# Moving a convolution's norm and a branch's product along a stick-breaking attention kernel, with some sums done by accumulating DMA

## The chip, the cores and the metric

The kernel runs on one core of a Trainium2 chip. The metric is device time in microseconds (us), the median over runs of one launch. The engines are called by their names in the profile: PE (TensorE, matrix products), DVE (VectorE), ACT (ScalarE), POOL (GpSimd) and SP (SyncE, which here only issues DMAs). All times are of the whole launch or of places in the span of one profiled execution.

## The reference, cut

One layer on `x` of 2048 rows by 1024 channels: a layer norm, one wide product with `w_in` into nine blocks of 1024 columns, then two branches that meet.

```python
h = _layer_norm(x, ln_in_g, ln_in_b)
q, k, v, z_sb, c_val, c_gate, z_cv, g_sb, g_cv = split(h @ w_in)          # 9 x 1024 columns
# branch s: 16 heads of 64; A[t,s] = sigmoid(l_ts) * prod_{s<j<t} (1 - sigmoid(l_tj)), s < t
y_sb = (attention(q, k, v) * silu(z_sb)) @ w_sb_proj
# branch c: causal depthwise convolution of 31 taps, layer norm over channels
u = conv(c_val * sigmoid(c_gate), conv_w, conv_b)
y_cv = (silu(_layer_norm(u, conv_ln_g, conv_ln_b)) * silu(z_cv)) @ w_cv_proj
merged = sigmoid(g_sb) * y_sb + sigmoid(g_cv) * y_cv
out = _layer_norm(ALPHA * h + merged @ w_out, ln_g, ln_b)
```

## The kernel before, in words

The rows are turned end to start, so that the attention's running products go forward; they are held as four chunks of 512 rows. Half 1 is chunks 3 and 2, half 0 chunks 1 and 0. Channels lie on the 128 partitions, in eight blocks. Every fp32 operand of a product is split into a high part `hi` (ScalarE, `activation` Copy to fp32r, L116) and a low part `lo` (VectorE, source minus `hi`, L117), and a product is three matmuls, `hi*hi`, `hi*lo`, `lo*hi`. A piece of work for PE in the fill lists is two of eight blocks of the contraction, so six matmuls of 512 columns; four pieces make one tile of 128 x 512, and `block` is two such tiles, one for each chunk of a half.

The first phase computes most column blocks of `h @ w_in` by a scheme of seven products in place of eight (L909). Its work comes in groups of 14 pieces: `order(h)` lists them, 36 groups for half 1 and 20 for half 0. A group `u` gives the gated input of one channel block of the convolution; when both chunks are there, `gated` queues a convolution (a generator of 51 steps, 45 of them taps of VectorE at L409) on the list `slow`.

`slow_step` is called after every piece. It adds `PACES[phase]` to a counter and, where the counter has reached 1, runs one step of the first convolution in the list, at a priority lowered by 800.

The convolution's norm is `conv_mean(h)` (mean over channels by a product with `ones`) and `conv_ln(c)`: for each of eight channel blocks subtract the mean, square and sum (`s2`, L467 to L474), then the inverse root through POOL (`m2`, `m3`), then scale, SiLU and the gate (`s3`, L501 to L505), into `acv`.

The second phase is the attention of eight pairs of heads, for half 1 and then for half 0, woven with a list of fill pieces: for each pair `k`, `q`, `v` and the gate `z` of half 0 (`fill_qkv`, `gate_z`), then branch `s` of half 1, then branch `c` of half 1. `weave_attention` orders the attention's items: logits (L583, L584), sigmoid (L586), a scan on VectorE (L589), a turn (four transposes at L612, split by L116 and L117), the product with `v` (L628). `SPLIT` is the share of the fill that lies beside half 1's attention, and `END` the number of entries of the fill that are left when the attention's last item has been issued. `done` closes a head: it sums the two halves of the partitions (L642), adds `v` (L648), multiplies by the gate (L649) and stores into `asb`.

The tail runs branch `s` of half 0, the output rows of chunks 3 and 2, branch `c` of half 0, and the output rows of chunks 1 and 0. `pair` interleaves the first two and last two blocks of a branch and lets `freed` start the loads of the next operands; `load_w` loads and splits a block's weights, or reads back split parts where an earlier pass has stored them (`wdr`). `soon` and `delay` put an item into the fill after a number of further entries.

Issue order on PE is the program's order. The other engines' order is made by the scheduler from priorities, but each engine then runs its own queue in order. All DMAs are issued from SP's queue.

The branch's end, as it stands (L707 to L717):

```python
def use(c, ps, g, *a):
    o = st()
    nc.vector.tensor_tensor(out=o, in0=ps, in1=g, op=ALU.mult)
    for a_ in a:
        nc.vector.tensor_tensor(out=o, in0=o, in1=a_, op=ALU.add)
    dma((mdr if a else pdr)[c, m], o)
```

Of the kernel before, what the change touches and what calls it, by code (L numbers as in the profile page):

```python
# [27 lines left out]
NBW = 4  # L28
LEAD = 4.0
LAG = 3  # L30
PACES = [0.78, 1.25, 0.6]
I0 = 1
SPLIT = 0.27
RD = 9
W1 = 5
END = 14
W0 = 3
N1 = 2
O0 = 25
O1 = 5  # L40
B0 = 62
# [13 lines left out]
def layer_kernel(ctx: ExitStack, tc, x, w_in, w_sb, w_cv, w_out, vecs, cw, rows, out):  # L55
# [32 lines left out]
    def dram(shape, dt, name):  # L88
        return tc.dram_tile(shape, dt, name=name)
# [7 lines left out]
    asb = {(c, m): dram([P, CH], F32, f"asb{c}_{m}") for c, m in CM}  # L97
    acv = {(c, m): dram([P, CH], F32, f"acv{c}_{m}") for c, m in CM}
    mdr = {(c, m): dram([P, CH], F32, f"mdr{c}_{m}") for c, m in CM}
    pdr = {(c, m): dram([P, CH], F32, f"pdr{c}_{m}") for c, m in CM}  # L100
    qdr = {(c, m): dram([2, P, CH], F32R, f"qdr{c}_{m}") for c, m in CM}
    kdr = {(c, m): dram([2, P, CH], F32R, f"kdr{c}_{m}") for c, m in CM}
    vtd = {(c, m): dram([P, CH], F32, f"vtd{c}_{m}") for c, m in CM}
# [40 lines left out]
    def load_w(src, col):  # L144


        hi, lo = (wp.tile([P, KB, P], F32R, name="w4", bufs=4) for _ in range(2))
        for g in range(2):
            ks = slice(g * 4, g * 4 + 4)
            if (id(src), col, g) in wdr:  # L150
                for t, e in ((hi, 0), (lo, 1)):
                    dma(t[:, ks], wdr[id(src), col, g][:, e])
                continue
            raw = wp.tile([P, 4, P], F32, name="wraw", bufs=2)
            nc.sync.dma_start(out=raw, in_=src[col // P][:, ks])
            split(raw, hi[:, ks], lo[:, ks])
        return hi, lo

    class Fill:
# [83 lines left out]
    def half(h):  # L243
        return (2 * h + 1, 2 * h)
# [268 lines left out]
    def attention(at, kv, lg_p, pv_p):  # L513
# [123 lines left out]
        def done(i, a, c, ps, hs, ls):  # L637
            if a == 0:
                sums[c] = at.tile([P, CH], F32, name="og", bufs=2)
            g, s = sums[c], st()  # L640
            nc.scalar.activation(s[hs], ps[ls], AF.Copy)
            nc.vector.tensor_tensor(out=g[hs], in0=ps[hs], in1=s[hs], op=ALU.add)  # L642
            if a == 0:
                return
            v, z = st(), st()
            dma(v, vtd[c, i])
            dma(z, gat[c, i, "b"])
            nc.vector.tensor_tensor(out=g, in0=g, in1=v, op=ALU.add)  # L648
            nc.vector.tensor_tensor(out=g, in0=g, in1=z, op=ALU.mult)  # L649
            dma(asb[c, i], g)  # L650

# [41 lines left out]
    def branch(n, h):  # L693

        def gate(m):
            def load(c):
                g = sg_p.tile([P, CH], F32, name="gt", bufs=2)
                dma(g, gat[c, m, n])
                return g
            return load  # L700

        def other(m):
            def load(c):
                a = st()
                dma(a, pdr[c, m])
                return a
            return load  # L707

        def use(m):
            def use(c, ps, g, *a):  # L710
                o = st()
                nc.vector.tensor_tensor(out=o, in0=ps, in1=g, op=ALU.mult)  # L712
                for a_ in a:
                    nc.vector.tensor_tensor(out=o, in0=o, in1=a_, op=ALU.add)
                dma((mdr if a else pdr)[c, m], o)
            return use

        src, bys = (w_sb, [gate]) if n == "s" else (w_cv, [gate, other])
        return [(src, m * P, [(c, lambda c=c: acts[n, c]) for c in half(h)], use(m)) + tuple(b(m) for b in bys)
                for m in range(KB)]  # L720

    srcs = {"s": asb, "c": acv, "m": mdr}
# [18 lines left out]
    def first_phase(F, x2, w1, ps_p):  # L741
# [255 lines left out]
            return g  # L997

        def order(h):
            us_ = [("u", m) for m in range(KB)]  # L1000
            rest = [(e, m) for m in range(4) for e in ("kqvzcgh" if h else "cgh")]
            out_ = []
            for n, u in enumerate(us_):
                out_.append(u)
                out_ += rest[len(rest) * n // 8:len(rest) * (n + 1) // 8]
            return out_

        groups = [group(1, *o) for o in order(1)] + [group(0, *o) for o in order(0)]
        rows, one, two = first_rows()
# [9 lines left out]
        later_rows()  # L1019
        prev, prev_g = None, None  # L1020
        for n, g in enumerate(groups):
            nxt = groups[n + 1] if n + 1 < len(groups) else None
            last = nxt is None or nxt["h"] != g["h"]
            first = n == 0
# [123 lines left out]
    with ExitStack() as s2:  # L1148
        kv = s2.enter_context(tc.tile_pool(name="kv", bufs=2))
        at = s2.enter_context(tc.tile_pool(name="at", bufs=2))  # L1150
        lg_p = s2.enter_context(tc.tile_pool(name="lgp", bufs=2, space=PS))
        pv_p = s2.enter_context(tc.tile_pool(name="pvp", bufs=2, space=PS))
        head = attention(at, kv, lg_p, pv_p)

        def gate_z(m):
            return w_in, COL_Z + m * P, xs(0), silu_to(m, "b")

        for i in range(NPAIR):
            ready[1, i] = True
        norm = conv_mean(1) + conv_ln(3) + conv_ln(2)  # L1160
        for i in range(NPAIR):
            fill_qkv(F, 0, i)
            if i < NPAIR - 2:
                F.block(*gate_z(i))
            for q in range(10):
                if norm and i >= I0:
                    F.delay(1 + 3 * q, 0.1, norm.pop(0))
        F.pair(gate_z(NPAIR - 2), gate_z(NPAIR - 1), freed=loads("s", 1))
        F.soon([(0.1, it) for it in norm], 1, 2)
        run(F, branch("s", 1), loads("c", 1))  # L1170
        F.soon([(0.1, it) for it in conv_mean(0) + conv_ln(1) + conv_ln(0)], N0, N1)
        run(F, branch("c", 1), loads("s", 0))
        end = len(F.pieces) - END
        steps, spans = [], []
        mid = int(end * SPLIT)
        for h, lo, hi in ((1, 0, mid), (0, mid, end)):
            spans += [(lo + (hi - lo) * i // NPAIR, lo + (hi - lo) * (i + 1) // NPAIR) for i in range(NPAIR)]
            for i in range(NPAIR):
                for a in range(2):
                    steps += [((0 if h else NPAIR) + i, st_) for st_ in head(i, a, h)]  # L1180
        pair_of = [p_ for p_, _ in steps]
        items = weave_attention([st_ for _, st_ in steps])
        work = {}
        for n, _, (cost, _) in items:
            work[pair_of[n]] = work.get(pair_of[n], 0) + cost
        seen = {}
        at_fill = 0
        for n, own, (cost, fn) in items:
            p_ = pair_of[n]
            lo, hi = spans[p_]  # L1190
            k = seen.get(p_, 0)
            seen[p_] = k + cost
            at_fill = max(at_fill, lo + int((hi - lo) * k / work[p_]))
            emit_fill(at_fill)
            o_ = pair_of[own]
            while (1 - o_ // NPAIR, o_ % NPAIR) not in ready:
                at_fill = n_done[0] + 1
                emit_fill(at_fill)
            fn()


    with ExitStack() as s2:
# [72 lines left out]
                            F.soon(freed)  # L1275

        run(F, branch("s", 0), loads("m", 1))
        output(F, 3, loads("c", 0)[0])
        output(F, 2, loads("c", 0)[1])
        run(F, branch("c", 0), loads("m", 0))  # L1280
        output(F, 1, ())
        output(F, 0, ())
        assert not F.later
# [34 lines left out]
```

## Time and profile before

| | |
|---|---|
| median of 3 runs | 3145.14 us (3144.13 to 3145.33) |
| the profiled execution | 3146.49 us |
| its span, first to last instruction | 3144.7 us |
| mean granted clock of PE | 0.978 |
| PE, DVE, ACT, POOL busy | 2896.8, 2603.8, 1414.0, 75.4 us |
| DMA moved, mean | 604.98 MB, 192 GB/s |

A row of a group in the profile reads: line, engine, operation, output and inputs by the program's names with their shape, count, then busy time in us and mean duration of one in ns, then the idle time of the engine just before, and what ended it. A row of a window reads: stretch, its length, and for each engine the busy time with the number of instructions, then the granted clock, the DMA share and GB/s. A row of waits reads: who waited for whom, us in total, times, the longest.

### The profile page before, as it was taken

To read this page: it belongs to the slowest core of one execution; us is meant where nothing else is said; L and a number is where in the kernel's file an instruction comes from. 1 tells how busy PE (TensorE), PEld (TensorE's weight loads), DVE (VectorE), ACT (ScalarE), POOL (GpSimd) and SP (SyncE) were. 2 spreads that over 40 slices of the span, in tenths; PEclk is the share of its full clock that TensorE was granted. 3 is DMA by queue.
4 is the path that set the end of the run, shared out by engine and by line. 5 is a ranking of instruction groups with operands and counts; after the bars stand their busy time and mean duration, and the time that the engine had idled before them with its cause. 6 is when DMAs were issued, how large, how long until landed. Compare 5 with 4: busy or idle time off the path is not lost.

```text
span 3144.7 us, 42164 instructions
## 1 busy us (share of the span) xinstructions
PE 2896.8 (92%) x14666; PEld 2402.7 (76%) x14666; DVE 2603.8 (83%) x3537; ACT 1414.0 (45%) x2582; POOL 75.4 (2%) x162
## 2 busy tenths in 40 slices
PE   6998999999999998899889889998899888879998
PEld 4776787878788886787777778887788777767887
DVE  8988989888777865998999988888988898856746
ACT  6553444444422323444454554555645555543322
POOL 1000000000000000000000000000000000000000
PEclk8999999999999999999999999999999999989999
DMA  5878757577865567555563454444543553486552
GB/s 179 301 232 307 264 194 267 206 264 282 286 222 185 176 228 218 169 182 176 182 185 119 149 172 134 156 146 140 167 129 118 158 180 120 145 288 231 169 187 81
DMA packets 319269, 604.98 MB, mean 192 GB/s; under 512 B 37456, under 2 KB 79568, under 8 KB 318928
## 3 DMA queue, kind: packets, MB, share of 16 engines
q1 hardware_dynamic: 319056, 602.29, 58.3%
q8 instruction: 115, 1.88, 0.3%
q14 instruction: 98, 0.80, 0.1%
HBM read 355.74 MB, written 246.42 MB: 191 GB/s over the span
## 4 chain that ended last, share of the span: by engine, by line
PE 47%; DVE 25%; issue 12%; DMA 7%; ACT 3%; SPq 1%; POOL 1%; DVEq 0%; POOLq 0%; ACTq 0%
PE pb L909 11%; PE mm L201 10%; DVE nb L589 10%; PE pp L909 7%; PE mm L909 7%; DVE tl L117 4%; PE tp L612 4%; PE pv L628 3%; PE lg L583 1%; DVE cy L409 1%; PE lg L584 1%; ACT th L116 1%; DVE cu L409 1%; ACT nb L586 1%; DMA st<-fdr 1%
## 5 line engine op out<-in xcount | busy, mean ns | idle before, releaser
L116 ACT ACTIVATE th<-tp 128x512 fp32r<-128x512 f32 (+1 forms) x576 | 329.6, 573 | 467.8 <-PE tp L612 459.2
L117 DVE TENSOR_TENSOR tl<-tp,th 128x512 fp32r<-128x512 f32 (+1 forms) x576 | 374.2, 652 | 92.2 <-ACT th L116 89.1
L612 PE MATMUL tp<-ident,nb 128*128 128x128 f32 x2176 | 354.6, 279 | 80.4 <-DVE nb L589 63.5
L586 ACT ACTIVATE nb<-lg 128x512 f32<-128x512 f32 (+3 forms) x640 | 331.3, 532 | 115.7 <-PE lg L584 114.0
L589 DVE TENSOR_TENSOR_SCAN nb<-nb,dd 128x256 f32<-128x256 f32 (+7 forms) x256 | 343.8, 1348 | 18.0 <-ACT nb L586 18.0
L628 PE MATMUL pv<-tl,v 128*128 128x256 f32 (+1 forms) x1152 | 303.1, 292 | 53.2 <-DVE tl L117 52.5
L612 PEld LDWEIGHTS tp<-ident,nb 128*128 128x128 f32 x2176 | 255.2, 142 | 116.7 <-DVE nb L589 78.8
L589 DVE TENSOR_TENSOR_SCAN nb<-nb,zero 128x1024 f32<-128x1024 f32 x128 | 300.1, 2347 | 23.3 <-ACT nb L586 23.1
L628 PE MATMUL pv<-th,v 128*128 128x256 f32 (+1 forms) x1152 | 307.8, 285 | 2.8 <-ACT th L116 2.6
L583 PE MATMUL lg<-k,qd 128*128 128x512 f32 (+3 forms) x640 | 267.9, 420 | 23.7 <-ACT nb L586 11.7
L628 PEld LDWEIGHTS pv<-tl,v 128*128 128x128 f32 x1152 | 219.1, 190 | 91.7 <-DVE tl L117 76.4
L628 PEld LDWEIGHTS pv<-th,v 128*128 128x128 f32 x1152 | 219.7, 191 | 20.5 <-ACT th L116 4.5
L584 PE MATMUL lg<-k,ql 128*128 128x512 f32 (+3 forms) x640 | 234.7, 367 | 0.0
L201 PE MATMUL mm<-A11h,w 128*128 128x512 f32 x512 | 185.6, 409 | 12.7 <-ACT w L116 7.0
L409 DVE SCALAR_TENSOR_TENSOR cy<-cu,csum,cy 128x512 f32<-128x512 f32 x240 | 179.2, 747 | 18.9 <-ACT cy L405 15.8
L201 PE MATMUL mm<-A12h,w 128*128 128x512 f32 x512 | 188.0, 413 | 0.0
L201 PE MATMUL mm<-SXh,w 128*128 128x512 f32 x512 | 182.8, 403 | 2.1 <-DVE st L712 2.1
L201 PE MATMUL mm<-A22h,w 128*128 128x512 f32 x512 | 182.7, 403 | 0.0
L409 DVE SCALAR_TENSOR_TENSOR cu<-cd,cwt,cu 128x512 f32<-128x512 f32 x240 | 179.1, 746 | 3.7
L409 DVE SCALAR_TENSOR_TENSOR cy<-cu,cwt,cy 128x512 f32<-128x512 f32 x240 | 179.1, 746 | 2.6
L583 PEld LDWEIGHTS lg<-k,qd 128*128 128x128 f32 x640 | 122.5, 191 | 48.7 <-ACT nb L586 29.0
L584 PEld LDWEIGHTS lg<-k,ql 128*128 128x128 f32 x640 | 123.7, 193 | 8.8 <-issue 0.2
(251 smaller groups left out, 6298.9 us busy)
## 6 DMA issues: line engine op xcount, KB each, us to landing
wdr<-w4x SPq DMA_DIRECT2D x78, 512.0 KB, 3.4
wdr<-w SPq DMA_DIRECT2D x68, 512.0 KB, 3.2
w4x<-wdr SPq DMA_DIRECT2D x52, 512.0 KB, 4.7
wraw<-in_w_in SPq DMA_DIRECT2D x100, 256.0 KB, 3.5
w<-wdr SPq DMA_DIRECT2D x96, 256.0 KB, 3.8
k<-kdr SPq DMA_DIRECT2D x192, 128.0 KB, 3.0
v<-vdr SPq DMA_DIRECT2D x96, 256.0 KB, 3.0
w<-wdr SPq DMA_DIRECT2D x46, 512.0 KB, 4.4
```

Of the source, the lines that this page charges most:

```text
L116: nc.scalar.activation(hi, src, AF.Copy)
L117: nc.vector.tensor_tensor(out=lo, in0=src, in1=hi.bitcast(F32), op=ALU.subtract)
L201: nc.tensor.matmul(box["ps"], lhsT=l[:, kb], rhs=r[kb], start=(kb == 0 and n == 0), stop=(kb == KB - 1 and n == 2))
L409: nc.vector.scalar_tensor_tensor(out=dst, in0=src[:, j:j + HN], scalar=t, in1=first, op0=ALU.mult, op1=ALU.add)
L583: nc.tensor.matmul(lg[:, :w], lhsT=qd[c][:, js], rhs=k2[kc][:, ko:ko + w], start=True, stop=False)
L584: nc.tensor.matmul(lg[:, :w], lhsT=ql[c][:, js], rhs=k2[kc][:, ko:ko + w], start=False, stop=True)
L586: nc.scalar.activation(nb[:, o:o + w], lg[:, :w], AF.Sigmoid, scale=-QS)
L589: nc.vector.tensor_tensor_scan(out=nb[:, :w], data0=nb[:, :w], data1=dd[:, :w] if diag else zero.to_broadcast([P, w]), initial=0.0 if diag ...
L612: nc.tensor.transpose(out=tp[:, at_:at_ + P], in_=tiles[j][:, so:so + P], identity=ident)
L628: nc.tensor.matmul(o[:, :w], lhsT=lv, rhs=tt[:, o0:o0 + w], start=(diag and t == 0 and n == 0 and e == 0), stop=(last and t == nt - 1 and ...
L909: nc.tensor.matmul(bank, lhsT=wt[:, e, kb], rhs=xs_[kb][a], start=start and kb == 0 and n == 0, stop=kb == 3 and n == 2, skip_group_check= ...
```

## The change

Six things change.

1. The norm of half 1 (`conv_mean(1)`, `conv_ln(3)`, `conv_ln(2)`, 70 items) is put into the first phase, from group 45 of 56 on, one item every second entry. Before, it was spread over the `k`, `q`, `v` and `z` blocks of the second phase. The norm of half 0 is now put before branch `s` of half 1 rather than after it, one item for every entry.
2. In `order`, the groups `u` come earlier: three other groups between two of them for half 1 and one for half 0. `PACES` for half 0 in the first phase is 1.6 in place of 1.25.
3. Branch `c` of half 0 is run in the fill beside the attention, after branch `c` of half 1. In the tail branch `s` of half 0 is followed by all four chunks of output rows.
4. `load_w` makes the low part with a ScalarE copy of `-hi` and a DMA from POOL's queue that adds the source to it, and stores the parts of `w_sb` and `w_cv` in DRAM at their first use, so that half 0 reads them back.
5. `done` adds `v` by an accumulating DMA from POOL's queue into the tile, ahead of the multiplication by the gate.
6. The two branches meet by an accumulating DMA into `mdr` in DRAM; the tensor `pdr`, its loads and its addition on VectorE are gone.

```diff
-PACES = [0.78, 1.25, 0.6]
-I0 = 1
+PACES = [0.78, 1.6, 0.6]
 SPLIT = 0.27
+NORM = 45
-END = 14
+END = 18
-N1 = 2
+N1 = 1
...
             raw = wp.tile([P, 4, P], F32, name="wraw", bufs=2)
             nc.sync.dma_start(out=raw, in_=src[col // P][:, ks])
-            split(raw, hi[:, ks], lo[:, ks])
+            nc.scalar.activation(hi[:, ks], raw, AF.Copy)
+            nc.scalar.activation(lo[:, ks], hi[:, ks].bitcast(F32), AF.Copy, scale=-1.0)
+            nc.gpsimd.dma_start(out=lo[:, ks], in_=src[col // P][:, ks].bitcast(F32R), accum_op=ALU.add)
+            if src is not w_in:
+                d = wdr[id(src), col, g] = dram([P, 2, 4, P], F32R, f"wdr{len(wdr)}b")
+                dma(d[:, 0], hi[:, ks])
+                dma(d[:, 1], lo[:, ks])
...
-            v, z = st(), st()
-            dma(v, vtd[c, i])
+            z = st()
+            nc.gpsimd.dma_start(out=g, in_=vtd[c, i], accum_op=ALU.add)
             dma(z, gat[c, i, "b"])
-            nc.vector.tensor_tensor(out=g, in0=g, in1=v, op=ALU.add)
             nc.vector.tensor_tensor(out=g, in0=g, in1=z, op=ALU.mult)
...
-            def use(c, ps, g, *a):
+            def use(c, ps, g):
                 o = st()
                 nc.vector.tensor_tensor(out=o, in0=ps, in1=g, op=ALU.mult)
-                for a_ in a:
-                    nc.vector.tensor_tensor(out=o, in0=o, in1=a_, op=ALU.add)
-                dma((mdr if a else pdr)[c, m], o)
+                if n == "sc"[h == 0]:
+                    dma(mdr[c, m], o)
+                else:
+                    nc.gpsimd.dma_start(out=mdr[c, m], in_=o, accum_op=ALU.add)
...
-            us_ = [("u", m) for m in range(KB)]
             rest = [(e, m) for m in range(4) for e in ("kqvzcgh" if h else "cgh")]
+            n = 3 if h else 1
             out_ = []
-            for n, u in enumerate(us_):
-                out_.append(u)
-                out_ += rest[len(rest) * n // 8:len(rest) * (n + 1) // 8]
-            return out_
+            for m in range(KB):
+                out_ += [("u", m)] + rest[m * n:m * n + n]
+            return out_ + rest[KB * n:]
...
         for n, g in enumerate(groups):
+            if n == NORM:
+                F.soon([(0.1, it) for it in conv_mean(1) + conv_ln(3) + conv_ln(2)], 1, 2)
...
-        norm = conv_mean(1) + conv_ln(3) + conv_ln(2)
...
-            for q in range(10):
-                if norm and i >= I0:
-                    F.delay(1 + 3 * q, 0.1, norm.pop(0))
         F.pair(gate_z(NPAIR - 2), gate_z(NPAIR - 1), freed=loads("s", 1))
-        F.soon([(0.1, it) for it in norm], 1, 2)
+        F.soon([(0.1, it) for it in conv_mean(0) + conv_ln(1) + conv_ln(0)], N0, N1)
         run(F, branch("s", 1), loads("c", 1))
-        F.soon([(0.1, it) for it in conv_mean(0) + conv_ln(1) + conv_ln(0)], N0, N1)
-        run(F, branch("c", 1), loads("s", 0))
+        run(F, branch("c", 1), loads("c", 0))
+        run(F, branch("c", 0), loads("s", 0))
...
         run(F, branch("s", 0), loads("m", 1))
-        output(F, 3, loads("c", 0)[0])
-        output(F, 2, loads("c", 0)[1])
-        run(F, branch("c", 0), loads("m", 0))
+        output(F, 3, loads("m", 0)[0])
+        output(F, 2, loads("m", 0)[1])
         output(F, 1, ())
         output(F, 0, ())
```

More of the change, by code (lines that the diff above doesn't have):

```diff
@@ L99, in layer_kernel @@
     mdr = {(c, m): dram([P, CH], F32, f"mdr{c}_{m}") for c, m in CM}
-    pdr = {(c, m): dram([P, CH], F32, f"pdr{c}_{m}") for c, m in CM}
     qdr = {(c, m): dram([2, P, CH], F32R, f"qdr{c}_{m}") for c, m in CM}
@@ L700, in gate @@
             return load
[L702 to L707, printed above, removed]
         def use(m):
-            def use(c, ps, g, *a):
+            def use(c, ps, g):
                 o = st()
                 nc.vector.tensor_tensor(out=o, in0=ps, in1=g, op=ALU.mult)
-                for a_ in a:
-                    nc.vector.tensor_tensor(out=o, in0=o, in1=a_, op=ALU.add)
-                dma((mdr if a else pdr)[c, m], o)
-            return use
-        src, bys = (w_sb, [gate]) if n == "s" else (w_cv, [gate, other])
-        return [(src, m * P, [(c, lambda c=c: acts[n, c]) for c in half(h)], use(m)) + tuple(b(m) for b in bys)
+                if n == "sc"[h == 0]:
+                    dma(mdr[c, m], o)
+                else:
+                    nc.gpsimd.dma_start(out=mdr[c, m], in_=o, accum_op=ALU.add)
+            return use
+        return [(w_sb if n == "s" else w_cv, m * P, [(c, lambda c=c: acts[n, c]) for c in half(h)], use(m), gate(m))
                 for m in range(KB)]
```

## The prediction

> **What bounds the kernel now.** I read the totals first, then the windows cut at the three joints of the program (the second half of the channels starts in the first phase at 794 us, attention starts at 1180 us and ends at 2735 us), then the waits inside each stage, then the priced groups.
>
> ```profile
> PE 2896.8 (92%) x14666; PEld 2402.7 (76%) x14666; DVE 2603.8 (83%) x3537; ACT 1414.0 (45%) x2582; POOL 75.4 (2%) x162
> ```
>
> ```profile
> core 0: us, PE busy (x) PEld busy (x) DVE busy (x) ACT busy (x) POOL busy (x), PEclk, DMA share, GB/s
> 0.00:794.00 794.00, 740.46 (x3226) 596.67 (x3226) 692.40 (x1112) 368.34 (x665) 37.90 (x81) 0.98 0.72 250
> 794.00:1180.00 386.00, 383.07 (x1654) 311.80 (x1655) 299.86 (x435) 114.25 (x192) 0.00 (x0) 1.00 0.66 218
> 1180.00:2735.00 1555.00, 1393.98 (x8166) 1186.87 (x8166) 1353.09 (x1598) 801.77 (x1547) 19.59 (x33) 0.98 0.51 158
> 2735.00:3145.00 410.00, 379.25 (x1623) 307.40 (x1621) 258.45 (x394) 129.61 (x179) 17.90 (x48) 0.96 0.57 188
> ```
>
> TensorE (PE) is the bound: 2897 of 3145 us. Its 248 us of idle time lie unevenly: 54 before 794, 3 until 1180, 161 beside attention (PE 89.6% busy, VectorE 87%), 31 in the tail. So the attention stage is the only one where much can be won, and the tail and the end of the first phase have VectorE (DVE) to spare: 152 and 86 us.
>
> ```profile
> PE tp L612 <- DVE nb L589: 63.5, 58, 4.4
> ...
> PE pv L628 <- DVE tl L117: 52.3, 76, 2.6
> ...
> PE tp L612 <- DVE tl L117: 16.3, 14, 2.2
> ```
>
> These are PE's waits beside attention: 132 of the 161 us are for VectorE, for a scan (L589) or for the low half of a split (L117). VectorE takes its work in order, and whatever else stands in its queue makes these two late. The next rows show that: the 29 windows of 50 us between 1230 and 2680 us, of which I set the eight with least VectorE work (all of those under 42 us) against the nine with most (all above 46). The least and the most loaded of each set:
>
> ```profile
> 2080.00:2130.00 50.00, 48.31 (x300) 42.05 (x299) 37.44 (x40) 24.18 (x47) 1.91 (x3) 1.00 0.34 108
> ...
> 1830.00:1880.00 50.00, 42.83 (x240) 35.64 (x240) 41.86 (x50) 27.88 (x51) 0.00 (x0) 0.97 0.49 158
> ```
> ```profile
> 1380.00:1430.00 50.00, 46.18 (x274) 40.11 (x274) 46.20 (x63) 24.72 (x52) 1.79 (x3) 0.97 0.57 180
> ...
> 1530.00:1580.00 50.00, 45.55 (x270) 38.99 (x269) 48.47 (x67) 26.10 (x55) 1.17 (x1) 0.97 0.62 195
> ```
>
> The eight average 46.9 us of PE (94%), the nine 44.3 (88%). The scatter is wide, but the direction is plain.
>
> **The change, part by part.** VectorE's prices, from the groups by shape:
>
> ```profile
> L117 DVE TENSOR_TENSOR w<-wraw,w 128x512 fp32r<-128x512 f32 x80 | 53.9, 684 | 15.9 <-ACT w L116 11.5 <-PE tp L612 3.3 <-PE lg L584 1.0
> L712 DVE TENSOR_TENSOR st<-mm,gt 128x512 f32<-128x512 f32 x64 | 43.9, 685 | 53.1 <-PE mm L201 52.9
> L714 DVE TENSOR_TENSOR st<-st 128x512 f32<-128x512 f32 x32 | 22.0, 687 | 0.4
> L505 DVE TENSOR_TENSOR st<-st 128x512 f32<-128x512 f32 x32 | 22.4, 700 | 0.4
> L648 DVE TENSOR_TENSOR og<-og,st 128x512 f32<-128x512 f32 x32 | 21.7, 680 | 3.4 <-DMA st<-vtd 3.4
> L501 DVE TENSOR_TENSOR st<-st,mu 128x512 f32<-128x512 f32 x32 | 21.9, 684 | 10.2 <-DMA st<-ydq 10.0
> L504 DVE TENSOR_TENSOR st<-st 128x512 f32<-128x512 f32 x32 | 21.9, 686 | 7.2 <-ACT st L503 7.1
> L467 DVE TENSOR_TENSOR st<-st,mu 128x512 f32<-128x512 f32 x32 | 21.7, 682 | 5.1 <-DMA st<-ydr 5.0
> L474 DVE TENSOR_TENSOR sum<-sum,st 128x512 f32<-128x512 f32 x28 | 19.2, 685 | 2.5 <-ACT st L469 2.0
> ```
>
> *The norm of half 1 moves into the first phase* (from group 45 on). Each of its 16 pieces (2 column blocks, 8 channel blocks) costs VectorE five of these operations (L467, L474, L501, L504, L505; one of 700 ns, four near 684): 3.44 us, 55 us in all, and its 80 DMAs on SP's queue. Group 45 is the tenth of the twenty after 794 us, so it lands at about 968 us.
>
> ```profile
> 968.00:1091.00 123.00, 123.00 (x537) 100.37 (x536) 92.19 (x135) 35.80 (x60) 0.00 (x0) 1.00 0.59 188
> 968.00:1180.00 212.00, 212.00 (x922) 172.84 (x921) 152.95 (x219) 53.48 (x89) 0.00 (x0) 1.00 0.64 206
> ```
>
> VectorE has 59 us free there and gets 55: 98%. The 70 items come one every second entry, at 22 entries a group of 19 us, so in some 123 us; in these they are 45% of VectorE beside the 75% of the upper row, which only fits because the convolution's steps are emitted at low priority and can slide. The DMAs come as close: 80 x 256 KB are 21 MB, 170 GB/s in 123 us, beside 188. A busy stretch of the first phase:
>
> ```profile
> 800.00:850.00 50.00, 48.33 (x209) 38.94 (x208) 42.07 (x63) 20.43 (x35) 0.00 (x0) 1.00 0.88 303
> ```
>
> 303 GB/s at a share of 0.88 is 344 at full share; 358 asked for 123 us needs 5 us more, and PE was at 97% here, so 3% of 212 us, 6 more. A norm on a loaded VectorE also made PE wait 5.8 us for its sum in the tail (quoted below); twice that is 12. PE waits for nothing in this stretch now, so no gain is possible: 0 to 23 us, I take **+12 us**, the middle.
>
> *The convolution.* One call of `slow_step` runs one step whatever the pace, so 1.25 and 1.6 both mean one step for each piece.
>
> ```profile
> 0.00:794.00 794.00, 251.79 (x337) 0.98 0.72 250
> 794.00:1180.00 386.00, 189.95 (x257) 1.00 0.66 218
> 1180.00:2735.00 1555.00, 104.68 (x142) 0.98 0.51 158
> ```
>
> These are the taps (L409) by stage. At 14 pieces for each group the twenty groups allow 280 steps, and a convolution is 51 steps of which 45 are taps: 247, near the 257 seen. I therefore expect the same 142 taps (105 us) to stay beside attention; taking `u` groups earlier only hands out work that waits anyway. Cost 0; were VectorE free to take the steps at 1.6, the stage after would lose those 105 us, which is a bound for the better.
>
> *Beside attention, VectorE* loses the 55 us; 48 weight splits (16 of `w_in`, 16 of `w_sb`, 16 of `w_cv`; the other 32 were the second loads for half 0, now read back ready) x 684 = 33; the sum L648, 32 x 680 = 22; the sum L714 for half 1, 16 x 687 = 11. It gains the branch `c` of half 0, 16 products (L712) and 16 splits, 22 us, and the remaining quarter of half 0's norm that now runs after 2735 us (8 of 32 pieces), 28 us. Net **-71 us**: 1353 becomes 1282. ScalarE gets 48 more copies for the weights and loses the norm's; at 52% busy it covers that. If it did not, 48 copies of about 0.6 us would be 30.
>
> *PE* gains the 64 pieces of that branch:
>
> ```profile
> 3000.00:3100.00 100.00, 100.00 (x436) 81.53 (x435) 58.18 (x89) 24.21 (x34) 4.19 (x12) 1.00 0.46 153
> ```
>
> 436 wide matmuls in 100 us are 229 ns each; 64 x 6 x 0.229 = 88 us. PE's work beside attention becomes 1394 + 88 = 1482. With VectorE near 81% of the stage, I take the 94% of the less loaded windows: 1482 / 0.94 = 1577, **+22 us**. The ends: idle time unchanged at 161 us gives 1643 (+88); a stage that shrinks by what VectorE loses gives 1484 (-71), which is PE's own work. 94% lies between, and it is what rows of this stage show.
>
> *The accumulating transfers.* 48 for weights, 32 for the sum with `v` before L649, 32 into `mdr`, all on POOL's queue, where before there was no DMA. Nearest rows: a load of the same 256 KB takes 3.1 us (`v`) to 4.0 us (`ydq`).
>
> ```profile
> st<-vtd SPq DMA_DIRECT2D x32, 256.0 KB, 3.1
> ...
> st<-ydq SPq DMA_DIRECT2D x32, 256.0 KB, 4.0
> ```
>
> The Trainium skill, page "DMA: Bandwidth & Descriptors", section on the anatomy of a DMA from GpSimd, fits 2.0 us plus size over 436 GB/s; an estimate from it is 2.6 us, and no run here shows a DMA from that queue yet. A weight part now comes one transfer later, some 3 to 4 us, but is asked for about six pieces ahead, at 1555 us for 384 pieces (eight of `k`, `q`, `v`, `z` with eight pieces each, and two branches of 64), so 4 us a piece. Only in the second block of a `pair` (five of them) is it two pieces, 8 us, against 4 + 0.6 + 0.6 + 4 = 9: 0 to 5 us each, I take **+4 us** in all. The writes into `mdr` are read a branch later; they cost nothing unless they delay other transfers, and the DMA share is 0.51. In `done` the product L649 now waits for the transfer; a row of the same shape, L501 behind its load, lost VectorE 10 us in 32, because other work is put between. I take 0 and price the failure below. Behind POOL's waiting DMAs stand only the small operations for `v` and the norm; POOL is 2% busy.
>
> *The tail* gives up the same 64 pieces, -88 us, and its start loses what held PE there:
>
> ```profile
> PE mm L201 <- DVE st L712: 7.8, 2, 5.7
> PE mm L201 <- ACT w L116: 7.0, 2, 6.2
> PE mm L483 <- DVE sum L474: 5.8, 1, 5.8
> ```
>
> The waits for a weight split and for the norm's sum, 13 us, have no cause left there; the longer way of the last head's sum (3 to 4 us) is covered by the 18 entries left to run instead of 14. **-12 us.**
>
> Sum against the profiled execution's own 3146.5 us (its span 3144.7 and 1.8 around it): +12 +22 +4 -88 -12 = -62, so 3084.5; the median of the runs is 1.4 lower, so **3083 us**.
>
> **The rivals.**
>
> *A, VectorE waits for the accumulating transfer (slower).* L649 stands in an in-order queue behind a DMA that can start only when L642 is done. If the schedule leaves too little between them, VectorE stands still with the scans behind it. SP suffers too, for the store of the result waits at the head of its queue, already
>
> ```profile
> SPq L93 <- DVE og L649: 118.2, 30, 12.9
> ```
>
> and loads for the next head stand behind. It decides from 71 / 32 = 2.2 us a time: then VectorE's load is back where it was, PE stays at 89.6%, 1482 / 0.896 = 1654, and the total is 3146 + 12 + 99 + 4 - 88 - 12 = 3161. At 3.5 us each it is some 40 more. For it: the transfer is 3 to 4 us long. Against it: L501.
>
> The Trainium skill, page "SBUF — State Buffer", section "SBUF: two separate sides", would make this worse: while VectorE runs an operation that uses both its ports on one operand, GpSimd cannot write the descriptors of its DMAs. By that rule the copies would hold an accumulation back; the page infers that two-input operations do not, and nearly all of VectorE's here are such. I leave the chance of A as the rows give it.
>
> *B, nothing is hidden.* The 161 us are chains of fixed length that more PE work does not fill: 1643 for the stage, 3146 + 12 + 88 - 88 - 12 = 3146, no change. Against it: the two sets of windows.
>
> *C, VectorE is the true bound.* The stage follows VectorE down: 1484 plus some stalls. Full effect 3146 + 12 - 71 - 100 = 2987; half of the way from my value, 3035. For it: PE's busy time contains the ends of matmuls that were held up, so its floor is lower than 1482.
>
> *D, the first phase chokes.* Norm and convolution ask for 120% of VectorE while the norm runs, and the transfers for all of the DMA engines. If the convolution does not slide, its 24 us stand before PE, and if the weights of the groups come late on top of the 23 us above, the price is about 47 instead of 12: 3118. For it: the sums; against it: the stretch of 89 us behind the norm, where VectorE has a third free.
>
> **How the numbers follow.** A measurement here tells 0.2%, 6 us, from no change. My case (3055 to 3108) 0.53; A 0.13; B 0.07; C (2990 to 3055) 0.15; D (3108 to 3138) 0.12. Leaving out A and the far end of C gives 3030 to 3135 for eight in ten. Faster: 0.53 + 0.15 + 0.12 = 0.80; same, B, 0.07; slower, A, 0.13.
>
> **What would show it.** Right: attention's stage still about 1580 us long with 1480 of PE in it, the waits of `tp` for scans and of `pv` for splits together under 80 us instead of 116, no norm (L467 to L505) after attention, a tail of about 310 us. The first phase's norm would show in 968 to 1100 us, with VectorE above 95% and PE near 98%. Taps after the first phase: 142, or my reading of the pace is wrong. Wrong: VectorE idle in front of the product in `done` for tens of us, PE waiting for a weight's low part, or a first phase that ends after 1200 us.

## The result, and the profile after

The changed kernel takes 3198.45 us (3196.19 to 3200.16, four runs) against 3144.64 for the kernel before: slower, ratio 1.0172, 95% interval 1.0154 to 1.0190. The prediction said 3083, in a range from 3030 to 3135. The first phase is taken to end where the last product into `pb` starts, and the attention stage where the last product into `pv` starts; before, these were at 1192.5 and 2741.0 us, after at 1258.2 and 2890.4. The totals of the profile after, then the busy times by stage, before and after:

```profile
span 3194.4 us, 42225 instructions
...
PE 2907.5 (91%) x14666; PEld 2419.0 (76%) x14666; DVE 2522.4 (79%) x3393; ACT 1425.7 (45%) x2598; POOL 177.2 (6%) x274
```
```profile
794.00:1192.00 398.00, 394.29 (x1701) 320.55 (x1702) 304.57 (x442) 116.72 (x196) 1.97 (x4) 1.00 0.66 217
1192.00:2741.00 1549.00, 1388.56 (x8158) 1183.22 (x8158) 1351.46 (x1595) 801.70 (x1547) 17.62 (x29) 0.98 0.50 157
2741.00:3145.00 404.00, 373.45 (x1585) 302.29 (x1583) 255.37 (x389) 127.22 (x175) 17.90 (x48) 0.96 0.57 191
```
```profile
core 0: us, PE busy (x) PEld busy (x) DVE busy (x) ACT busy (x) POOL busy (x), PEclk, DMA share, GB/s
0.00:794.00 794.00, 742.88 (x3238) 599.53 (x3239) 696.01 (x1118) 372.01 (x670) 38.90 (x81) 0.98 0.72 252
794.00:1258.00 464.00, 411.88 (x1729) 331.58 (x1728) 351.97 (x522) 149.35 (x243) 4.42 (x6) 0.94 0.71 232
1258.00:2890.00 1632.00, 1469.35 (x8494) 1259.31 (x8492) 1295.01 (x1487) 821.85 (x1581) 101.74 (x123) 0.97 0.58 168
2890.00:3194.00 304.00, 283.42 (x1209) 228.53 (x1209) 179.45 (x267) 82.52 (x105) 32.10 (x64) 0.98 0.54 171
```

VectorE lost 81 us of work and the kernel still became 54 us longer. The stages tell where: the tail is 100 us shorter, as forecast (404 to 304). The first phase ends 66 us later (1192.5 to 1258.2), and the attention stage is 84 us longer (1548.5 to 1632.2), no less than the 81 us of PE work that came into it (1388.6 to 1469.4): none of PE's idle time there was filled.

**In the first phase** the first row is PE's longest wait from 794 to 1192 us before; the next two are its longest from 950 us on after. Then comes the timeline around the longest, cut to the norm's last step (L506 to L510), SP's queue and the eviction L947:

```profile
PE pb L909 <- ACT st L950: 3.3, 1, 3.3
```
```profile
PE pb L906 <- ACT st L947: 34.2, 4, 15.8
PE mm L488 <- DVE sum L479: 10.4, 2, 5.7
```
```profile
1066.69 0.33 SPq L93 DMA_DIRECT2D acv<-st  x1
...
1068.05 0.53 SPq L93 DMA_DIRECT2D st<-ydq  x1
...
1072.70 0.69 DVE L510 TENSOR_TENSOR st<-st 128x512 f32<-128x512 f32 x1 [0.98 <-DMA st<-gat_5z]
...
1073.42 0.32 SPq L93 DMA_DIRECT2D acv<-st  x1
...
1077.04 0.53 SPq L93 DMA_DIRECT2D st<-ydq  x1
...
1081.17 0.81 ACT L507 ACTIVATE st<-st,vec 128x512 f32<-128x512 f32 x1 [3.83 <-DVE st L506]
...
1081.89 0.58 ACT L947 ACTIVATE st<-pb 128x512 f32<-128x512 f32 x1
...
1082.52 0.79 PE L906 MATMUL pb<-S3h,w4x 128*128 128x512 f32 x1 [15.79 <-ACT st L947]
```

A piece of the norm's last step comes every 6 us (acv stored at 1061.1, 1066.7, 1073.4 and 1078.8). SP stores a piece when VectorE's last product of it (L510) is done, and only then gets to the load of a later piece. ScalarE's L507 waits for that piece, and behind L507 in ScalarE's queue stands L947, which empties the bank that PE needs. So one queue's order turns the pieces into a round trip, and PE stands 15.8 us behind it.

This stop cost PE more than its length. In the 10 us around the stop's end PE's 21 products took 356 ns each, at a granted clock of 0.60; in the next 10 us they took 222 ns, at 1.00:

```profile
1080.00:1090.00 10.00, 7.48 (x21) 5.95 (x22) 8.09 (x13) 3.27 (x5) 0.00 (x0) 0.60 0.64 211
1090.00:1100.00 10.00, 10.00 (x45) 8.26 (x44) 8.58 (x14) 3.96 (x7) 0.00 (x0) 1.00 0.83 260
```

That is some 2.8 us lost after the stop. The 66 us of the first phase are 46 us more of idle time and 20 us more of busy time. Of the 20, the norm's own 36 products (L452, L488, L499) are 8.5; the remaining 11 or so fit the lower clock, 0.94 from 794 us on where it was 1.00.

**Beside attention** VectorE has a new wait, for the transfer that adds `v`:

```profile
DVE og L653 <- DMA og<-vtd: 33.0, 16, 4.5
DVE og L653 <- issue: 28.6, 13, 3.3
```
```profile
1435.18 0.69 DVE L647 TENSOR_TENSOR og<-pv,st 64x512 f32<-64x512 f32 x1
1435.92 0.69 DVE L116 TENSOR_TENSOR tl<-tp,th 128x512 fp32r<-128x512 f32 x1
1436.17 0.88 POOL L651 DMA_DIRECT2D og<-vtd  x1 [1.72 <-DVE og L647]
1436.53 2.02 DVE L594 TENSOR_TENSOR_SCAN nb<-nb,dd 128x896 f32<-128x896 f32 x1
1443.10 0.69 DVE L653 TENSOR_TENSOR og<-og,st 128x512 f32<-128x512 f32 x1 [4.55 <-DMA og<-vtd]
...
1444.37 0.68 DVE L116 TENSOR_TENSOR tl<-tp,th 128x512 fp32r<-128x512 f32 x1
...
1445.11 0.58 PE L633 MATMUL pv<-tl,v 128*128 128x256 f32 x1 [5.72 <-DVE tl L116]
```

VectorE finishes a scan at 1438.6 and stands 4.55 us before the product L653; the split that PE waits for (L116) is in the queue behind it, and PE stands 5.72 us. In all 61.6 us in 29 such waits, both rows together; the waits put down to "issue" count with the others, because they go too in the run where `v` is added by VectorE.

### The profile page after: what moved, and what is told of

Its sections match the earlier page's. It is cut to its first block, busy times and chain, and to the rows that moved or that the text cites. A ratio compares the mean times of both kernels' runs of the same rounds, so it can differ in the third digit from the quotient of the medians.

```text
span 3194.4 us, 42225 instructions
## 1 busy us (share of the span) xinstructions
PE 2907.5 (91%) x14666; PEld 2419.0 (76%) x14666; DVE 2522.4 (79%) x3393; ACT 1425.7 (45%) x2598; POOL 177.2 (6%) x274
## 4 chain that ended last, share of the span: by engine, by line
PE 52%; issue 17%; DVE 11%; DMA 10%; ACT 3%; POOL 1%; SPq 1%; POOLq 0%; DVEq 0%; ACTq 0%
PE mm L206 14%; PE pb L906 10%; PE mm L906 7%; PE pp L906 6%; PE pv L633 5%; PE tp L617 4%; DVE nb L594 3%; PE lg L588 2%; PE lg L589 2%; DMA og<-vtd 2%; DVE tl L116 2%; DMA st<-ydq 1%; SPq L93 1%; DVE cy L414 1%; DMA st<-acv 1%
## 5 line engine op out<-in xcount | busy, mean ns | idle before, releaser
L116 DVE TENSOR_TENSOR tl<-tp,th 128x512 fp32r<-128x512 f32 (+1 forms) x576 | 374.0, 652 | 142.7 <-ACT th L115 139.8
L206 PE MATMUL mm<-A11h,w 128*128 128x512 f32 x512 | 188.3, 411 | 10.1 <-DMA w<-wdr48b 4.7
```

The source lines that it names most:

```text
L116: nc.vector.tensor_tensor(out=lo, in0=src, in1=hi.bitcast(F32), op=ALU.subtract)
L206: nc.tensor.matmul(box["ps"], lhsT=l[:, kb], rhs=r[kb], start=(kb == 0 and n == 0), stop=(kb == KB - 1 and n == 2))
```

## The experiments

Times are medians, ratios are against the kernel before, which was timed beside each group at 3146 to 3148 us. The first phase, attention and tail columns are from each run's profiled execution, which lies up to 7 us from the median (norm_beside_attention: 3205 against 3198).

| run | us | ratio, 95% interval | first phase | attention | tail |
|---|---|---|---|---|---|
| before | 3145 | | 1192.5 | 1548.5 | 404 |
| changed | 3198 | 1.0154 to 1.0190 | 1258.2 | 1632.2 | 304 |
| norm_beside_attention | 3198 | 1.0145 to 1.0186 | 1192.3 | 1709.4 | 301 |
| v_sum_on_vector | 3153 | 1.0011 to 1.0031 | 1256.8 | 1591.9 | 302 |
| norm_spread | 3177 | 1.0079 to 1.0120 | 1237.8 | 1630.9 | 303 |
| eight_st_tiles | 3196 | 1.0132 to 1.0172 | 1258.2 | 1633.8 | 303 |
| norm_loads_ahead | 3161 | 1.0031 to 1.0062 | 1232.6 | 1627.0 | 303 |
| v_sum_and_spread | 3133 | 0.9944 to 0.9981 | 1240.4 | 1589.3 | 302 |
| c_in_tail_v_sum | 3173 | 1.0067 to 1.0111 | 1259.1 | 1528.6 | 384 |
| no_accumulating_dma | 3124 | 0.9901 to 0.9946 | 1240.4 | 1584.4 | 299 |
| product_later | 3154 | 1.0017 to 1.0048 | 1261.7 | 1593.0 | 302 |
| all_good_parts | 3108 | 0.9856 to 0.9893 | 1231.3 | 1574.1 | 298 |
| norm_beside_no_accum | 3127 | 0.9914 to 0.9961 | 1191.8 | 1631.7 | 298 |
| weights_accumulated | 3129 | 0.9916 to 0.9954 | 1232.6 | 1587.0 | 301 |
| repaired_change | 3119 | 0.9888 to 0.9934 | 1231.9 | 1583.9 | 303 |
| norm_beside_loads_ahead | 3101 | 0.9826 to 0.9883 | 1183.7 | 1619.9 | 298 |

**norm_beside_attention**: the norm of half 1 back in the second phase.

```diff
-            if n == NORM:
-                F.soon([(0.1, it) for it in conv_mean(1) + conv_ln(3) + conv_ln(2)], 1, 2)
+        norm = conv_mean(1) + conv_ln(3) + conv_ln(2)
+            for q in range(10):
+                if norm and i >= 1:
+                    F.delay(1 + 3 * q, 0.1, norm.pop(0))
```

> The changed kernel with one part undone: the norm of half 1 goes back to the k, q, v and z blocks of the second phase. Theory 1 (the norm costs the first phase its 66 us, because its chains of loads, VectorE and ScalarE steps go through the seven rotating st tiles that the groups' evictions also need): the first phase ends at about 1193 us again instead of 1258, and the attention stage grows by far less than that, 0 to 30 us; total 3135 to 3165. Rival 1a (the first phase lost its time to the earlier u groups or the higher pace): the first phase still ends near 1258 and the total is 3198 to 3230. Rival 1b (the norm only moves: it costs as much beside attention, VectorE being loaded there): first phase 1193, stage longer by 50 us or more, total 3185 to 3205.

Measured 3198: the first phase is back at 1192.3, so its whole loss is the norm's, and neither the earlier groups `u` nor the pace cost anything. But the attention stage took 77 us more (in an execution 6 us above the median). Theory 1's second half, that the norm is cheap there, fell; rival 1b stands.

**v_sum_on_vector**: `v` loaded by SP and added by VectorE.

```diff
-            nc.gpsimd.dma_start(out=g, in_=vtd[c, i], accum_op=ALU.add)
+            dma(v, vtd[c, i])
+            nc.vector.tensor_tensor(out=g, in0=g, in1=v, op=ALU.add)
```

> The changed kernel with one part undone: v is loaded and added by VectorE in done, not by the accumulating DMA. Theory 2 (VectorE's product in done stands 62 us in front of the transfer, 2.1 us each, with scans and splits queued behind it): the waits of og for vtd fall under 5 us, VectorE gets 22 us of sums back, and the attention stage shortens by 20 to 40 us; total 3158 to 3178. Rival 2 (PE's idle beside attention, 162 us, is a chain that does not depend on these stands): stage within 8 us, total 3190 to 3206.

Measured 3153: 45 us gone by this edit, 40 of them in the attention stage, as much as the most that I expected there; the total came out 5 us below the expected range. Of the 40, about 32 are idle time of PE and 8 its busy time for the same products. What is left of the wait, 9.5 us where I expected under 5:

```profile
DVE og L653 <- DMA st<-vtd: 9.5, 7, 3.3
```

**product_later** asks whether it is the wait or the transfer. The transfer stays; the product and its store come five turns later.

```diff
             nc.gpsimd.dma_start(out=g, in_=vtd[c, i], accum_op=ALU.add)
-            dma(z, gat[c, i, "b"])
-            nc.vector.tensor_tensor(out=g, in0=g, in1=z, op=ALU.mult)
-            dma(asb[c, i], g)
+            pend.append([5, close])      # close(): the three lines above; every turn counts it down
```

> The changed kernel with the accumulating transfer of v kept, but the product with the gate behind it and the store issued five turns later (some 14 us), so that the transfer has landed when VectorE reaches the product. Theory 2 in its narrow form (what costs is that VectorE stands in its own queue in front of a transfer of 4.6 us, 62 us in all, not the transfer itself): the waits of og for vtd fall under 8 us and the total comes to 3145 to 3168, as with the sum on VectorE. Rival 2b (the transfer costs as such, by POOL's queue, the DMA engines or the port that VectorE shares): the waits go, but the total stays at 3180 to 3203.

Measured 3154, attention 1593.0, the same as with the sum on VectorE. So the cost was the product standing behind the transfer, and not the transfer as such. Two things are not separated. SP's own wait for that product, to store its result, fell too: from 138 us to 93 with the sum on VectorE and to 62 here. And the transfer takes 20 us of work off VectorE in this stage without a gain, but the edit also moved the load of the gate (`gat`) next to its product. VectorE now stands 20 us for these loads, 26 with the row below, against 12 us in front of the sum and the product in v_sum_on_vector. That can account for 14 of the 20 us.

```profile
DVE og L656 <- DMA og<-vtd: 5.8, 2, 3.5
```

**norm_spread**: the norm from group 39 on, every fifth entry.

```diff
-NORM = 45
+NORM = 39
-conv_mean(1) + conv_ln(3) + conv_ln(2)], 1, 2)
+conv_mean(1) + conv_ln(3) + conv_ln(2)], 1, 5)
```

> The changed kernel with the same norm in the first phase, but from group 39 on and one item every fifth entry instead of from group 45 and every second (70 items over 350 entries instead of 140). Theory 1 (the norm was given out faster, one item in 1.8 us of pieces, than its chains through seven st tiles can run, 6 us for a piece of the last step): with room the loss shrinks to 0 to 25 us, first phase ends 1193 to 1220, total 3130 to 3165. Rival 1c (each item costs PE a fixed stall in the first phase, however spread): first phase still about 1258, total 3190 to 3205.

Measured 3177, first phase 1237.8: 20 of the 66 us. Density was part of it (the norm also starts earlier here); most of the loss stayed, beyond what theory 1 allowed.

**eight_st_tiles**:

```diff
-        return sg_p.tile([P, CH], dt, name="st", tag="st", bufs=7)
+        return sg_p.tile([P, CH], dt, name="st", tag="st", bufs=8)
```

> The changed kernel with eight st tiles in rotation instead of seven, nothing else. If the rotation of the st tiles is what holds the norm's chains and with them the evictions in the first phase, one more tile lets more of a third chain run: first phase 10 to 30 us shorter, total 3165 to 3188. If it is VectorE's or the DMA engines' load (120% asked for), the first phase stays within 8 us of 1258 and the total within 3185 to 3202.

Measured 3196, first phase 1258.2: nothing. The rotation of the tiles, which I had put into theory 1, does not hold the norm here. That left SP's order or the load.

**norm_loads_ahead**: eight tiles, and in both steps the loads of piece m+1 are issued before piece m is worked on.

```diff
         def s3(m):
-            y, s, z = st(), st(), st()
-            dma(y..., ydq[h, m][:, :, hs])
-            dma(z, gat[c, m, "z"])
+            y, z = box.pop(("q", m))
+            ld3(m + 1)                   # the two loads of the next piece
+            s = st()
```

> The changed kernel (norm from group 39... no: from group 45, every second entry, as changed) with eight st tiles, which alone did nothing, and with the norm's loads in both steps issued one item earlier. Theory 1b (in the changed kernel SP issues a piece's store, which waits for VectorE's last product, before the next piece's loads, so each piece of the norm's last step takes a whole round of load, five operations and store, 6 us, and the evictions behind them on ScalarE wait with them): the round is cut to about 4 us, first phase 1215 to 1240 instead of 1258, total 3155 to 3182. Rival (the load of VectorE and the DMA engines, 120% asked for): first phase within 8 us of 1258, total 3188 to 3203.

(It starts from group 45, every second entry.) Measured 3161, first phase 1232.6: 26 us of it, and the total 37 us less. SP's wait for L510, first in the changed kernel and then here (L523), both from 950 to 1258 us, and PE's wait for the same eviction (L960 here):

```profile
SPq L93 <- DVE st L510: 39.6, 16, 7.2
```
```profile
SPq L93 <- DVE st L523: 15.1, 9, 5.1
```
```profile
PE pb L919 <- ACT st L960: 13.2, 4, 5.4
```

PE's wait fell from 34.2 to 13.2 us with the same work in the same place (VectorE's is 349 us against 352). So the round of store before load is the cause of some 26 of the 66 us, and VectorE's load is not. The other 40 us are still there.

**v_sum_and_spread**: the edits of v_sum_on_vector and norm_spread together.

> The changed kernel with two edits that each moved it: v is added by VectorE in done, and the norm runs from group 39 on, every fifth entry. If the two costs are independent, the first phase ends near 1238 and the attention stage takes 1592 us: total 3130 to 3138 (3198 - 45 - 21 = 3132), faster than the kernel before. If they share a cause (the store in done and the norm's store both block SP's queue), the sum is less than the parts: 3140 to 3155.

Measured 3133, as the sum of the parts: the two costs are independent.

**c_in_tail_v_sum**: branch `c` of half 0 back in the tail.

```diff
-        run(F, branch("c", 1), loads("c", 0))
-        run(F, branch("c", 0), loads("s", 0))
+        run(F, branch("c", 1), loads("s", 0))
...
+        run(F, branch("c", 0), loads("m", 0))
```

> The kernel of v_sum_on_vector (3153 us) with one more part undone: branch c of half 0 goes back into the tail, behind the output rows of chunks 3 and 2, and END stays 18. Theory 3 (beside attention about half of its 88 us of PE work is hidden in PE's idle time): attention 1592 falls to 1540 to 1555, the tail grows by 88 to 100 us, total 3185 to 3208. Rival B (nothing hidden): attention near 1504, total 3148 to 3165. A result below 3148 would mean that the move costs.

Measured 3173 against 3153: the move is worth 19 us. The stage is 63 us shorter without it and the tail 82 longer, so a quarter of the branch was hidden beside attention, less than the half that I expected here; stage and total both came out below the expected ranges.

**no_accumulating_dma**: v_sum_and_spread with weights split and branches joined by VectorE.

```diff
-            nc.scalar.activation(lo[:, ks], hi[:, ks].bitcast(F32), AF.Copy, scale=-1.0)
-            nc.gpsimd.dma_start(out=lo[:, ks], in_=src[col // P][:, ks].bitcast(F32R), accum_op=ALU.add)
+            split(raw, hi[:, ks], lo[:, ks])
...
-                    nc.gpsimd.dma_start(out=mdr[c, m], in_=o, accum_op=ALU.add)
+                    nc.vector.tensor_tensor(out=o, in0=o, in1=a_, op=ALU.add)      # a_ from pdr
```

> The kernel of v_sum_and_spread with the other two accumulating transfers undone as well: the low parts of the weights by VectorE (48 operations, still stored and read back), and the branches joined through pdr by VectorE (32). VectorE gets about 55 us of work back, most of it beside attention; the 64 transfers on POOL's queue go. If these two are a gain for VectorE, as predicted: attention stage 5 to 30 us longer than in v_sum_and_spread, total 3135 to 3162. If the transfers cost through the DMA engines, SP's queue or late weights: the same or shorter, 3110 to 3132.

Measured 3124. VectorE got back 45 us of busy time, and the kernel is 9 us faster, the intervals just touching: leaving these sums to transfers was no gain for the kernel. **weights_accumulated** puts the weights' transfers back:

```diff
-            split(raw, hi[:, ks], lo[:, ks])
+            nc.scalar.activation(hi[:, ks], raw, AF.Copy)
+            nc.scalar.activation(lo[:, ks], hi[:, ks].bitcast(F32), AF.Copy, scale=-1.0)
+            nc.gpsimd.dma_start(out=lo[:, ks], in_=src[col // P][:, ks].bitcast(F32R), accum_op=ALU.add)
```

> The kernel of no_accumulating_dma with one of the transfers put back: the low parts of the weights by ScalarE and an accumulating DMA; v and the join of the branches stay on VectorE. It stands between no_accumulating_dma (3124) and v_sum_and_spread (3132), which has the join by accumulating DMA too. If the weights' transfers cost the 9 us between the two: 3130 to 3136. If the join's transfers do (6 us to land, 256 KB read and written in DRAM): 3120 to 3127.

Measured 3129, between the two, with intervals that overlap both: which of the two kinds costs is not told apart. One sign in the changed kernel is that SP stood 91 us beside attention until the weights' transfers had landed, to store the parts (38 for `w_sb`, 53 for `w_cv`); whether that cost time is not shown.

**all_good_parts**: no_accumulating_dma with the edits of norm_loads_ahead and eight_st_tiles.

> The kernel of no_accumulating_dma (3124 us: norm in the first phase from group 39, every fifth entry; no accumulating transfers; branch c of half 0 beside attention) with the norm's loads one item ahead and eight st tiles. Theory 1b: the first phase, 1240 us there, still holds rounds that wait for loads behind a store; loads ahead bring it to 1208 to 1228, total 3092 to 3112. Rival (spreading and loading ahead cure the same waits, so that nothing is left): first phase within 6 us of 1240, total 3117 to 3127.

Measured 3108; the gain is there (16 us), but only 9 of it in the first phase, which stays at 1231, above the expected 1228. So 39 of the 66 us remain with both cures: 23 of idle time and 16 of busy time. PE's longest waits after 794 us are now for VectorE's `gt` (11.9 us) and for the load in `conv_mean` (10.1 us). **repaired_change** is all_good_parts with all three kinds of transfer kept and the product five turns later:

> The changed kernel with all its accumulating transfers kept and its two faults repaired: the product in done five turns later, the norm from group 39 and every fifth entry with its loads one item ahead and eight st tiles. Against all_good_parts (3108), the same without the transfers. If moving 76 us of VectorE's sums into transfers is a gain once nothing waits for them: 3085 to 3103. If they only shift the load (POOL's queue, twice the DMA time for a byte): 3108 to 3125.

Measured 3119: with both faults mended the change beats the kernel before by 0.9% (0.66 to 1.12%), and without the transfers it is some 11 us better, with intervals that just touch. Here too VectorE stands 21 us for the gate's late loads, so this is not yet the transfers' best case.

**norm_beside_no_accum**: the edits of norm_beside_attention, v_sum_on_vector and no_accumulating_dma together, without the spread.

> The changed kernel without the three kinds of accumulating transfer and with half 1's norm beside attention as in the kernel before; what is left of the change are the branch beside attention, the order of the groups, the stored weights and END. Theory 1 in its first form said that the norm costs little beside attention; norm_beside_attention (3198) spoke against it, but with the transfers in place. If the norm's cost there came from VectorE standing before the transfers: first phase 1193, attention 1580 to 1610, total 3075 to 3105. If the norm costs as much beside attention as in the first phase: attention 1625 to 1660, total 3118 to 3155.

Measured 3127, the second branch: attention 1632, 47 us more than with the norm in the first phase (1584), and the first phase 49 less. The norm's place is indifferent at its present form. **norm_beside_loads_ahead** adds the loads ahead and eight tiles:

> The kernel of norm_beside_no_accum (3127; first phase 1192, attention 1632) with the norm's loads one item ahead and eight st tiles. Theory 1b for this place (SP holds the next loads behind a store there too): attention 1605 to 1622, total 3098 to 3117. Rival (there it is VectorE's load, 86% of the stage, and not the round): attention within 8 us of 1632, total 3119 to 3133.

Measured 3101, attention 1619.9, 12 us less, as expected if the round costs there too. But the eighth tile was not tried alone in this place, and the first phase, which has no norm here, fell by 8 us as well. So the tile may have a part in it; the two are not told apart. This is the fastest kernel here, 1.5% (1.17 to 1.74%) faster than before.

```profile
1184.00:2804.00 1620.00, 1471.41 (x8533) 1259.76 (x8533) 1396.21 (x1668) 832.29 (x1586) 22.49 (x30) 0.97 0.56 178
```

VectorE has 101 us more work in this stage than in the changed kernel, and the stage is 12 us shorter.

## Why the prediction was wrong, step by step

Three terms of the sum make up the 115 us between 3083 and 3198: the norm in the first phase (54 us off), the sum with `v` (40 to 45) and the branch (17).

*The accumulating transfers* (0 for the product L649): the term put at nothing, 40 to 45 us. I took the row of L501, which waits little behind its load, as the likeness. But that load can be issued early; this transfer starts only when L642 has written and lands 4.6 us after POOL starts on it (0.9 of them the issue), and the order had about one scan in between. It was rival A as written, at 61.6 / 32 = 1.9 us a time, a little under the 2.2 that I had given as its point. The Trainium skill, page "DMA: Bandwidth & Descriptors", section "Anatomy of one DMA — SWDGE (gpsimd) path", has a fit for GpSimd's DMAs, and an estimate from it is 2.6 us. The trace has 4.6 for the sum with `v`, 5.8 to 7.7 for the weights and 6.0 into `mdr`, and the measurement decides:

```profile
og<-vtd POOLq DMA_DIRECT2D x32, 256.0 KB, 4.6
...
mdr<-st POOLq DMA_DIRECT2D x32, 256.0 KB, 6.0
...
w<-in_w_in POOLq DMA_DIRECT2D x16, 256.0 KB, 6.1
```

The rule of the Trainium skill, page "SBUF — State Buffer", section "SBUF: two separate sides" (VectorE holding the descriptors back) was hardly put to a test, because nearly all of VectorE's operations here have two inputs. POOL's part took 865 to 1092 ns for the sum with `v`; for the weights of `w_cv` it took up to 1509 ns (median 1089), and no run shows why.

```profile
L651 POOL DMA_DIRECT2D og<-vtd x32: 865/875/1092, 1312.9 to 2892.3; - x32
```

*The norm in the first phase* (+12): measured +66, the term that was furthest off. Its bounds, 0 to 23, were made of VectorE's and the DMA engines' capacity. On average neither was full (VectorE 76% from 794 to 1258 us, DMA share 0.71), and the sign that I named, VectorE above 95% with PE near 98%, did not come: from 970 to 1100 us VectorE was busy 70% and PE 79%. Only PE's wait for the norm's sum was right, 10.4 us against 12. At nothing stood the order of SP's queue, which turned 16 pieces into rounds of 6 us with evictions behind them, although the count of 80 DMAs was there; PE's slower clock after a stop; and the norm's own 8.5 us of PE, put into a stretch where PE was full. norm_beside_attention shows that all 66 us are the norm's, and norm_loads_ahead that 26 are the round's; for the other 40 the waits are named above, but no run with the norm in this place takes them away, and their cause stays open. Rival D had the place right and the reason and size (+47) wrong.

*The branch beside attention* (+22): with `v` on VectorE the stage is 1592, so +43 in place of +26 (+22, and the +4 of the weights). PE's share came to 1462 / 1592 = 92% and not 94%: the windows that I compared may differ in more than VectorE's load. The waits for scans and splits that were to be under 80 us were 106, and 83 with `v` on VectorE. The direction held: c_in_tail_v_sum, with VectorE's relief and without the branch, has a stage 20 us shorter than before. VectorE's relief was 56 us (1351 to 1295) of the forecast 71.

*The tail* (-88 and -12): measured -99.7, as PE's busy time less 90 and its idle time less 10. The total is right in part by luck: the waits named for the -12 went, and 10 us for read-back weights came in their place. *The pace* (no effect): 138 taps ran after the first phase against 142, as forecast (a convolution has 46 on that line, not 45: 736 in 16). *The weights in pairs* (+4): nowhere did PE wait for a low part.

*The chances*: A and D were given as exclusive cases. They came together, and only together do they make 3198; A with my first phase would have been near 3145. The range also held less than I said: B, at 3146, lies outside it as A does, so it had 0.80 less the far end of C, and not eight in ten.

## What to carry to other kernels

Before giving a sum to a DMA, look at what is queued behind its reader. Here VectorE, which takes its work in order, stood up to 4.55 us with scans and splits behind, and 22 us of saved additions did not pay for it. Place the reader several items later (its other loads issued early, which no run here tried), or leave the sum where it is. And where one queue issues both loads and stores, look for a loop body written as load, work, store: once its pieces came close, here it became a round trip, and one load ahead took back 26 of the 66 us. A forecast made of capacities alone sees neither.

## What was not expected of the hardware

Accumulating transfers use the DMA engines about twice as long for a byte as the others: 5.7% of 16 engines' span for 29 MB, 57.0% for 602 MB, so 0.19 against 0.095% for a MB. All of them go by POOL's queue and all the others by other queues, so the runs do not tell whether the sum or the queue does it.

```profile
q1 hardware_dynamic: 319056, 602.29, 57.0%
q0 software_dynamic: 16128, 29.37, 5.7%
```

PE's clock after a stop was not in the forecast either: 0.60 in the 10 us around the end of the stop of 15.8 us, 1.00 in the 10 us after.

That an operation fewer on the fuller engine gained nothing, in product_later against v_sum_on_vector, was the other surprise. The gate's loads, which that edit made late, can account for 14 of the 20 us; the rest stays open.
